# Mixer weights of a hybrid layer: both rounded parts of each strip stored in scratch memory in the first block and loaded from there in the later blocks

## The chip, the cores and the metric

One core of a Trainium2 chip runs the whole kernel. The metric is device time in microseconds (us); lower is better. TensorE (PE) does the matmuls and VectorE (DVE), ScalarE (ACT) and GpSimd (POOL) the rest. SyncE's queue (SP) issues nearly all transfers, which 16 DMA engines carry.

## The reference, cut to what matters

A layer on 2048 tokens of width 1024, in float32: a normalisation, a projection by `w_in`, a convolution branch and a gated delta rule beside it, `w_out`, a feed-forward network and a last normalisation.

```python
h = adaln(x, g_norm_mix[layer], shift_m, scale_m)
p = h @ w_in[layer]                       # 1024 x 3592
gate_b, gate_c, h_conv, q, k, v, z, a, bt = jnp.split(p, split_at, axis=-1)
ya = gate_b * causal_depthwise_conv(gate_c * h_conv, conv_w_mix[layer])   # then a group norm
...                                       # q, k, v: convolution, silu, heads, l2 norm
o = chunked_gated_delta_rule(q, k, v, g_dec, beta)
y = jnp.concatenate([ya, yb], axis=-1) @ w_out[layer]
x = x + gate_m[:, None, :] * y
h = adaln(x, g_norm_ffn[layer], shift_f, scale_f)
gt, up = jnp.split(h @ w_gate_up[layer], 2, axis=-1)
x = x + gate_f[:, None, :] * ((jax.nn.silu(gt) * up) @ w_down[layer])
return adaln(x, g_norm_final, shift_o, scale_o)
```

## The kernel before, in words

**Products in parts.** A matrix product of float32 values is made of three matmuls in the type fp32r: each operand is cut into a rounded part `hi` and a rest `lo`, and hi·hi, hi·lo and lo·hi are summed in PSUM. Weights come in strips of 512 KB (128 partitions x 1024 values). `raw_w` (L382) loads a strip into `wraw` (4 buffers). `split_w` (L387) makes the two parts: ACT casts into `whi` (L389), DVE subtracts into `wlo` (L391). `whi` and `wlo` have 4 buffers each (the pool `wc`). The buffers of `wraw` also serve the modulation vectors (`mod_gen`, L460, which loads strips of `w_ada` one by one beside the other work, L465, and sums them on DVE, L467 and L469) and the second normalisation (`second_norm`, L579).

**The mixer.** It runs in 4 blocks of 512 tokens. A block uses 28 column strips of `w_in` (`col_strip`: k, q, v, z for four heads each, then 12 for the convolution branch), each for 24 matmuls of 512 columns in `proj` (L447), and then strips of `w_out` (`out_strip`): 8 of them in blocks 1 to 3, each for 24 matmuls. Block 0 goes through its 8 `w_out` strips twice, in two groups (`out_groups`, L406), with 12 matmuls a strip, so that the last two of its four token tiles come later. That is 152 strips in all, 36 of them different.

**Order of requests.** `requests` (L417) lists the strips of all four blocks. `next_w` (L443) keeps `PRE + 1` = 4 strips under way and hands out the first: when a strip is handed out, the third after it has been asked for. Block 0 begins apart: its first four strips are used a piece at a time, while the modulation of the next columns of the input is still being made from `w_ada` (`part_norm`, L798; `part_start`, L818; loads on L778; sums on DVE, L793 and L795; column sums on PE, L483).

**Order on the engines.** From the first k strip of block 0 to the end of the mixer, the order on each engine is planned: the class `Clock` (L54) follows all instructions with costs of its own, and `pin` (L201) fixes the order by the begin that it gives them. The chains of the delta rule (`head_chain`, `q_chain`, `chunk_chain`) and of the convolution branch (`mix_chain`, L1295; its cast is L1303) are put between the matmuls of the projections by it. An engine runs its instructions strictly in this order. SP too takes its transfers in order: one that waits for a buffer holds up all behind it.

**Behind the mixer** come the feed-forward network's two halves and its last product, with their own loads and splits. They have no pinned order.

Of the kernel before, what the change touches and what calls it, by code (L numbers as in the profile page):

```python
# [12 lines left out]
F32 = mybir.dt.float32  # L13
F32R = mybir.dt.float32r
# [6 lines left out]
P = 128  # L21
D = 1024
S = 2048
KD = D // P
# [186 lines left out]
def layer_kernel(ctx, tc, x, c, w_ada, b_ada, w_ada_final, b_ada_final, g_norm_mix, g_norm_ffn, g_norm_final,  # L211
                 w_in, conv_w_mix, conv_w_qkv, a_log, dt_bias, g_conv_out, g_dn_out, w_out, w_gate_up,
                 w_down, cst, out):
    nc = tc.nc
    x, out = x[0], out[0]
    w_ada, w_in, w_out, w_gate_up, w_down = w_ada[0], w_in[0], w_out[0], w_gate_up[0], w_down[0]
# [9 lines left out]
    wc = wctx.enter_context(tc.tile_pool(name="wc", bufs=4, side="left"))  # L226
    dr = ctx.enter_context(tc.tile_pool(name="dr", bufs=1, space=DRAM))
# [3 lines left out]
    def dense_ps():  # L231
        return pd.tile([P, 512], F32, name="pd")

    def misc_ps():
        return pm.tile([P, 512], F32, name="pm")
# [146 lines left out]
    def raw_w(src, shape, name="wraw"):  # L382
        raw = wr.tile(shape, F32, name=name)
        nc.sync.dma_start(raw, src)
        return raw

    def split_w(raw, shape):  # L387
        hi = wc.tile(shape, F32R, name="whi")
        nc.scalar.copy(hi, raw)  # L389
        lo = wc.tile(shape, F32R, name="wlo")  # L390
        (lo_engines.popleft() if lo_engines else nc.vector).tensor_sub(lo, raw, hi.bitcast(F32))  # L391
        return hi, lo
# [13 lines left out]
    def out_groups(b):  # L406
        if b:
            return [[(n, kp, range(CH)) for kp in KPS] for n in range(2)]
        return [[(n, kp, range(2 * g, 2 * g + 2)) for kp in order for n in range(2)]
                for g, order in enumerate((KPS, sorted(KPS)))]  # L410


    def strip_ahead():
        raw = [raw_w(w_gate_up[:, c0:c0 + P].rearrange("(k p) n -> p k n", p=P), [P, KD, P]) for c0 in (0, FF)]
        return raw, split_w(raw[0], [P, KD, P])

    def requests():  # L417
        for b in range(NB):
            for c0 in (2048, 1536, 2560, 3072):
                for h in range(NH):  # L420
                    yield col_strip, w_in, c0 + h * P
            for m in range(4):
                for c0 in (512, 1024, 0):
                    yield col_strip, w_in, c0 + m * P
            for g in out_groups(b):
                for n, kp, ts in g:
                    yield out_strip, n, kp
        yield strip_ahead,
    reqs, ready, bg = requests(), deque(), deque()

    def fill(n):
        while len(ready) < n:
            r = next(reqs, None)
            if r is None:
                break
            ready.append(r[0](*r[1:]))
            if bg:
                try:
                    next(bg[0])
                except StopIteration:  # L440
                    bg.popleft()

    def next_w():  # L443
        fill(PRE + 1)
        return ready.popleft()

    def proj(ps, w, hh, hl, ks=range(KD)):  # L447
        wh, wl = w
# [272 lines left out]
    with ExitStack() as actx:  # L721
# [29 lines left out]
        pre = []  # L751
# [64 lines left out]
                scale_split(ps, k, Gm, Sm, *hT)  # L816

        def part_start():  # L818
            pre.append((ready.popleft(), dense_ps()))
            clock.kept.add(pre[-1][1].name)  # L820

        def proj_ab(ps, ks):
# [7 lines left out]
        for h in range(NH):  # L830
            part_start()
            proj(pre[h][1], pre[h][0], *hT, ks=PARTS[0])
# [33 lines left out]
        for b in range(NB):  # L866
            hh, hl = hT
# [393 lines left out]
            for key, c0, dstT in (("k", 2048, kT), ("q", 1536, qT), ("v", 2560, None)):  # L1261
                clock.pinned = clock.pinned or key == "k"
                for h in range(NH):
                    m = (c0 - 1536) // P + h
                    if pre:
                        w, ps = pre.pop(0)
                        proj(ps, w, hh, hl, PARTS[2])
                        clock.kept.discard(ps.name)
                        fill(h + 1)
                    else:  # L1270
                        w, ps = next_w(), misc_ps() if b == 0 and key == "q" and h < 1 else dense_ps()
                        proj(ps, w, hh, hl)
                    take_now("cv", 1)
                    cv = cv_tile([P, BLK])
                    conv(cv, ps, [col["cw_qkv"][:, t * 12 + m:t * 12 + m + 1] for t in range(4)], halo[:, m, :])
                    nc.vector.tensor_copy(edge[:, m, :], ps[:, BLK - 3:])
                    nc.scalar.activation(cv if dstT is None else dstT[:, h, :], cv, AF.Silu)
                    done[key] += 1
                    if dstT is not None:
                        give("cv", 1)  # L1280
                    else:
                        spawn(v_chain(h, cv), 1)
# [4 lines left out]
            for h in range(NH):  # L1287
                w = next_w()
                ps = dense_ps()
                proj(ps, w, hh, hl)  # L1290
                nc.scalar.activation(zs[:, h, :], ps, AF.Silu)
                done["z"] += 1
# [26 lines left out]
            for m in range(4):  # L1319
                w = next_w()  # L1320
                pcg = dense_ps()
                proj(pcg, w, hh, hl)
                take_now("cv", 2)
                gc = cv_tile([P, BLK])
                nc.scalar.copy(gc, pcg)
                w = next_w()
                phc = dense_ps()
                proj(phc, w, hh, hl)
                nc.vector.tensor_mul(phc, phc, gc)
                give("cv", 1)  # L1330
                nc.vector.tensor_copy(uedge[:, m, :], phc[:, BLK - 2:])
                cv = cv_tile([P, BLK])
                conv(cv, phc, [col["cw_mix"][:, t * 4 + m:t * 4 + m + 1] for t in range(3)], uhalo[:, m, :])
                w = next_w()
                pgb = dense_ps()
                proj(pgb, w, hh, hl)
                nc.vector.tensor_mul(cv, cv, pgb)
                spawn(mix_chain(m, cv), 1)
# [288 lines left out]
    for hf in range(2):  # L1627
        m = 0
# [226 lines left out]
    for n, (g, s) in enumerate(items):  # L1855
# [9 lines left out]
        if g == 0:  # L1865
            for q in range(4):
                p = dense_ps()
                u, c0 = q // 2, q % 2
# [75 lines left out]
```

## Time and profile before

| what | value |
|---|---|
| time, median of 3 runs | 2406.51 us (2406.47 to 2407.99) |
| span of the profiled execution, first to last instruction | 2404.1 us |
| median less this span | 2.4 us |
| PE busy | 2342.0 us (97%) |
| DVE, ACT, POOL busy | 1779.7 (74%), 1050.3 (44%), 572.9 us (24%) |
| moved by DMA | 341.19 MB, mean 142 GB/s |

The span of the profiled execution is its own time; what lies around it in a run is the 2.4 us of the third row. A `group` row gives busy time and mean duration of one kind of instruction, and then how long its engine sat idle just before it and for whom. A `window` row gives, for a stretch of the span, its length and the busy time of PE, PE's weight loads, DVE, ACT and POOL with counts of instructions, then the granted TensorE clock (1.00 is full speed), the DMA engines' share and the rate. In a timeline, the row has start and duration, and in brackets the idle time before it and who ended it; "x8" is eight instructions merged.

### The profile page before, as it was taken

What the parts mean: (1) busy time and instruction counts of PE and PEld (TensorE: products, weight loads), DVE (VectorE), ACT (ScalarE), POOL (GpSimd) and SP (SyncE); (2) the same over time, 40 slices, a digit from 0 to 9 for tenths busy, and PEclk for the clock granted to TensorE, in tenths of its full rate; (3) what the DMA queues carried; (4) which work ended last, traced back from release to release, by engine and by line L of the source; (5) the groups of instructions that cost most, each with busy time, mean ns of one, the idle gap of its engine ahead of it and who ended that gap; (6) DMA issues with size and microseconds to landing.
All of it is one profiled execution on the core that took longest, in us unless ns stands there. A gap on an engine that the chain in (4) does not pass through costs nothing. (4 is left out here: it accounts for less than half of the span.)

```text
span 2404.1 us, 30949 instructions
## 1 busy us (share of the span) xinstructions
PE 2342.0 (97%) x11285; PEld 1938.6 (81%) x11285; DVE 1779.7 (74%) x2667; ACT 1050.3 (44%) x1787; POOL 572.9 (24%) x646
## 2 busy tenths in 40 slices
PE   7899999999999999999999999999999999999997
PEld 6788888887788888887888888878888877887786
DVE  5898879775977678788666556875656568878987
ACT  3644664444634564356543334433333323322345
POOL 0241344033513161111000000000000036434448
PEclk9999999999999999999999999999999999999999
DMA  7443565535553345255663334753433374333443
GB/s 252 119 119 92 169 191 164 148 106 166 145 141 122 115 141 146 61 155 161 215 209 116 101 104 122 247 161 90 129 99 105 104 247 154 121 108 119 136 138 142
DMA packets 400992, 341.19 MB, mean 142 GB/s; under 512 B 39796, under 2 KB 343165, under 8 KB 400775
## 3 DMA queue, kind: packets, MB, share of 16 engines
q1 hardware_dynamic: 399430, 337.01, 45.9%
q0 software_dynamic: 1152, 2.10, 0.6%
q8 instruction: 88, 1.44, 0.2%
q14 instruction: 66, 0.53, 0.1%
q10 hardware_dynamic: 256, 0.10, 0.0%
HBM read 265.74 MB, written 75.51 MB: 142 GB/s over the span
## 5 line engine op out<-in xcount | busy, mean ns | idle before, releaser
L389 ACT CAST whi<-wraw 128x1024 fp32r<-128x1024 f32 x286 | 299.7, 1049 | 394.1 <-PE pd L322 170.6
L391 DVE TENSOR_TENSOR wlo<-wraw,whi 128x1024 fp32r<-128x1024 f32 x286 | 360.3, 1261 | 102.7 <-ACT whi L389 100.0
L322 PE MATMUL pd<-hTh,whi 128*128 128x512 f32 x888 | 362.0, 409 | 0.6 <-ACT hTh L564 0.6
L322 PE MATMUL pd<-hTh,wlo 128*128 128x512 f32 x888 | 348.4, 392 | 1.0 <-DVE wlo L391 1.0
L322 PE MATMUL pd<-hTl,whi 128*128 128x512 f32 x888 | 348.2, 392 | 0.1
L322 PEld LDWEIGHTS pd<-hTh,wlo 128*128 128x128 f32 x888 | 167.7, 189 | 38.2 <-DVE wlo L391 1.4
L322 PEld LDWEIGHTS pd<-hTh,whi 128*128 128x128 f32 x888 | 168.5, 190 | 33.6 <-issue 1.0
L322 PEld LDWEIGHTS pd<-hTl,whi 128*128 128x128 f32 x888 | 168.3, 190 | 32.1 <-issue 1.0
L1606 POOL TENSOR_TENSOR wraw<-wraw 128x1024 f32<-128x1024 f32 x2 | 4.9, 2458 | 776.0 <-DMA wraw<-in_w_down_dram 776.0
L1554 DVE TENSOR_TENSOR sg<-sg,pd 128x512 f32<-128x512 f32 x44 | 30.2, 686 | 163.1 <-PE pd L322 163.1
L1812 DVE TENSOR_TENSOR acc<-acc,pd 128x512 f32<-128x512 f32 x192 | 127.3, 679 | 24.6 <-PE pd L322 23.8
L1692 ACT CAST xh<-ra 128x640 fp32r<-128x640 f32 (+1 forms) x85 | 60.4, 722 | 183.0 <-PE pm L322 137.3
L1239 DVE SCALAR_TENSOR_TENSOR cv<-pd,pcb,cv 128x511 f32<-128x511 f32 (+2 forms) x173 | 129.4, 748 | 5.2
L1701 POOL TENSOR_TENSOR xl<-ra,xh 128x640 fp32r<-128x640 f32 (+1 forms) x37 | 62.7, 1695 | 143.9 <-ACT xh L1692 133.7
L1812 DVE TENSOR_TENSOR acc<-acc,pm 128x512 f32<-128x512 f32 x120 | 81.6, 680 | 17.7 <-PE pm L322 17.2
L322 PE MATMUL pd<-whi,ym 128*128 128x512 f32 x256 | 84.8, 396 | 0.0
L1741 POOL TENSOR_TENSOR wraw<-wraw 128x512 f32<-128x512 f32 x40 | 68.8, 1743 | 47.1 <-DMA wraw<-in_w_down_dram 39.7
L322 PE MATMUL pd<-A22h,whi 128*128 128x512 f32 x176 | 68.9, 391 | 3.0 <-DVE sg L1554 3.0
L322 PE MATMUL pm<-S4h,whi 128*128 128x512 f32 x176 | 68.6, 390 | 1.4 <-ACT sg L1548 1.4
L322 PE MATMUL pd<-S2h,whi 128*128 128x512 f32 x176 | 68.6, 390 | 1.0 <-ACT whi L389 1.0
L322 PE MATMUL pd<-S2h,wlo 128*128 128x512 f32 x176 | 68.6, 390 | 0.5 <-DVE wlo L391 0.5
L322 PE MATMUL pd<-S3h,t3h 128*128 128x512 f32 x176 | 69.0, 392 | 0.0
(459 smaller groups left out, 6207.2 us busy)
## 6 DMA issues: line engine op xcount, KB each, us to landing
wraw<-in_w_in_dram SPq DMA_DIRECT2D x112, 512.0 KB, 4.6
wraw<-in_w_gate_up_dram SPq DMA_DIRECT2D x88, 512.0 KB, 3.9
ra<-act SPq DMA_DIRECT2D x80, 448.0 KB, 3.6
wraw<-in_w_out_dram SPq DMA_DIRECT2D x40, 512.0 KB, 3.6
act<-S SPq DMA_DIRECT2D x80, 256.0 KB, 3.5
act<-act SPq DMA_DIRECT2D x68, 256.0 KB, 2.7
wraw<-in_w_ada_dram SPq DMA_DIRECT2D x32, 512.0 KB, 4.2
wraw<-in_w_down_dram SPq DMA_DIRECT2D x22, 512.0 KB, 4.3
```

The source lines that it names most:

```text
L322: mm(*args, **kw)
L389: nc.scalar.copy(hi, raw)
L391: (lo_engines.popleft() if lo_engines else nc.vector).tensor_sub(lo, raw, hi.bitcast(F32))
L1239: nc.vector.scalar_tensor_tensor(cv[:, n - t:], u[:, :BLK - n + t], taps[t], cv[:, n - t:], op0=ALU.mult, op1=ALU.add)
L1554: nc.vector.tensor_add(s5[i], s5[i], a[i])
L1606: nc.gpsimd.tensor_mul(r, r, first_w["gate"])
L1692: nc.scalar.copy(hi, raw[:, c0:c1, :])
L1701: eng.tensor_sub(lo, raw, hi.bitcast(F32))
L1741: nc.gpsimd.tensor_mul(r[:, hs], r[:, hs], gate_f[:, hs])
L1812: nc.vector.tensor_add(accs[s, u][:, ns], accs[s, u][:, ns], ps)
```

## The change

In block 0 each of the 36 strips is still loaded, cast and subtracted. When it is handed out, both parts are also written to scratch memory in DRAM (`put_by`, two stores of 512 KB). Whenever a strip comes again, in block 0's second `w_out` group and in blocks 1 to 3, `part_load` loads the two parts straight into `whi` and `wlo`: no raw strip, no cast and no subtraction, and two loads of 512 KB instead of one. Both kinds of transfer are issued on SP. The first four strips are stored in `part_start`. The feed-forward network's weights are left as they were.

```diff
+    def part_load(key):
+        tiles = []
+        for name, src in zip(("whi", "wlo"), parted[key]):
+            t = wc.tile([P, D], F32R, name=name)
+            nc.sync.dma_start(t.bitcast(F32), src)
+            tiles.append(t)
+        return tiles
+
+    def parts_of(key, make, *args):
+        k, n = (KD, P) if make is col_strip else (2, 512)
+        if key in parted:
+            return [t.rearrange("p (k n) -> p k n", n=n) for t in part_load(key)]
+        tiles = make(*args)
+        parted[key] = [dr.tile([P, D], F32, name=f"parted{len(parted)}_{e}") for e in "hl"]
+        stores[id(tiles)] = tiles, parted[key]
+        return tiles
...
-                    yield col_strip, w_in, c0 + h * P
+                    yield parts_of, c0 + h * P, col_strip, w_in, c0 + h * P
...
-                    yield out_strip, n, kp
+                    yield parts_of, (n, kp), out_strip, n, kp
...
+    def put_by(w):
+        tiles, dst = stores.pop(id(w), ((), ()))
+        for t, d in zip(tiles, dst):
+            nc.sync.dma_start(d, t.rearrange("p k n -> p (k n)").bitcast(F32))
+        return w
+
     def next_w():
         fill(PRE + 1)
-        return ready.popleft()
+        return put_by(ready.popleft())
...
-            pre.append((ready.popleft(), dense_ps()))
+            pre.append((put_by(ready.popleft()), dense_ps()))
```

The lines behind L412 stand 24 to 27 lines later in the changed kernel (L778 becomes L805, L1303 becomes L1330). The stores are L467 there, the loads of parts L419.

The order moves at three places. The first is SP's queue in the first microseconds, before the pinned order begins: behind the four raw strips stood the `w_ada` loads for the second part of the modulation (`yah`, `yal` and `ym` are the buffers that they go to).

```order
L384 DMA wraw<-in_w_in_dram 128x8x128 x4
L778 DMA yah<-in_w_ada_dram 128x384 x4
L778 DMA yal<-in_w_ada_dram 128x384 x4
L778 DMA ym<-in_w_ada_dram 128x384 x8
L836 DMA wab<-in_w_in_dram 128x8x8
```

In the changed kernel the eight stores of the first four strips stand between them (`parted_h` and `parted_l` are the scratch tensors of the two parts).

```order
L384 DMA wraw<-in_w_in_dram 128x8x128 x4
L467 DMA parted_h<-whi 128x1024
L467 DMA parted_l<-wlo 128x1024
L467 DMA parted_h<-whi 128x1024
L467 DMA parted_l<-wlo 128x1024
L467 DMA parted_h<-whi 128x1024
L467 DMA parted_l<-wlo 128x1024
L467 DMA parted_h<-whi 128x1024
L467 DMA parted_l<-wlo 128x1024
L805 DMA yah<-in_w_ada_dram 128x384 x4
L805 DMA yal<-in_w_ada_dram 128x384 x4
L805 DMA ym<-in_w_ada_dram 128x384 x8
```

The sixteen `w_ada` loads are now issued only when DVE has made the fourth strip's `wlo`.

The second place is ACT in block 1, at the first cast of the convolution branch (`lv<-cv`, L1303 before). Before, casts of strips (`whi<-wraw`) stand all around it.

```order
L389 CAST whi<-wraw 128x1024 x2
L1301 ACTIVATE cv<-cv 128x512
L389 CAST whi<-wraw 128x1024
L1325 COPY cv<-pd 128x512
L389 CAST whi<-wraw 128x1024
L1303 CAST lv<-cv 128x512
L389 CAST whi<-wraw 128x1024
L1310 ACT_TABLE_LOAD
```

Now (L1330) none of them is left, and the delta rule's last copies (`lv<-pm`) have come ahead of it.

```order
L1352 COPY cv<-pd 128x512
L1103 COPY lv<-pm 128x512 x4
L1119 COPY lv<-pm 64x4x64 x4
L1128 COPY lv<-pm 64x4x64 x4
L1239 ACTIVATE junkd,so<-ch 128x128 x4
L1328 ACTIVATE cv<-cv 128x512
L1330 CAST lv<-cv 128x512
```

So on ACT nothing here waits for a weight strip any more, and the planner has chosen another order for the chains.

The third place is SP's queue at block 0's second `w_out` group. Before, the raw strips (`wraw`) stand ahead of the block's results (`x_0` and `x_1` are token tiles of the result in DRAM, `cb` is a piece of the input).

```order
L384 DMA wraw<-in_w_out_dram 128x2x512 x7
L1392 DMA x_0_107<-cv 128x512
L1387 DMA cb<-in_x_dram 128x512
L1392 DMA x_1_108<-cv 128x512
L1387 DMA cb<-in_x_dram 128x512
L384 DMA wraw<-in_w_out_dram 128x2x512
L1392 DMA x_0_107<-cv 128x512
```

Now most of the loads of parts, each of which waits until PE has let go of a buffer, stand between the results.

```order
L1419 DMA x_0_107<-cv 128x512
L1414 DMA cb<-in_x_dram 128x512
L419 DMA whi<-parted_h 128x1024
L419 DMA wlo<-parted_l 128x1024
L1419 DMA x_1_108<-cv 128x512
L1414 DMA cb<-in_x_dram 128x512
L419 DMA whi<-parted_h 128x1024 x2
L419 DMA wlo<-parted_l 128x1024 x2
L419 DMA whi<-parted_h 128x1024
L419 DMA wlo<-parted_l 128x1024 x2
L1419 DMA x_0_107<-cv 128x512
```

A load of parts now waits for results of DVE and POOL that stand ahead of it, and the results wait for PE.

More of the change, by code (lines that the diff above doesn't have):

```diff
@@ L410, in out_groups @@
                 for g, order in enumerate((KPS, sorted(KPS)))]
+    parted = {}
+    def part_load(key):
[13 more added lines that the diff above has]
+        return tiles
+    stores = {}
     def strip_ahead():
@@ L420, in requests @@
                 for h in range(NH):
-                    yield col_strip, w_in, c0 + h * P
+                    yield parts_of, c0 + h * P, col_strip, w_in, c0 + h * P
             for m in range(4):
                 for c0 in (512, 1024, 0):
-                    yield col_strip, w_in, c0 + m * P
+                    yield parts_of, c0 + m * P, col_strip, w_in, c0 + m * P
             for g in out_groups(b):
                 for n, kp, ts in g:
-                    yield out_strip, n, kp
+                    yield parts_of, (n, kp), out_strip, n, kp
         yield strip_ahead,
```

## The prediction

> **What bounds the kernel now.** I read the busy times first, then stretches of the span, then PE's waits. The page says that PE is the bound, and what one strip's two parts cost on the other engines:
>
> ```profile
> span 2404.1 us, 30949 instructions
> PE 2342.0 (97%) x11285; PEld 1938.6 (81%) x11285; DVE 1779.7 (74%) x2667; ACT 1050.3 (44%) x1787; POOL 572.9 (24%) x646
> ...
> L389 ACT CAST whi<-wraw 128x1024 fp32r<-128x1024 f32 x286 | 299.7, 1049 | 394.1 <-PE pd L322 170.6
> L391 DVE TENSOR_TENSOR wlo<-wraw,whi 128x1024 fp32r<-128x1024 f32 x286 | 360.3, 1261 | 102.7 <-ACT whi L389 100.0
> ```
>
> The windows split the span at about the ends of the start, of block 0, and of the mixer:
>
> ```profile
> 0.00:45.00 45.00, 28.19 (x119) 24.68 (x120) 22.21 (x45) 18.35 (x27) 4.81 (x17) 0.97 0.90 290
> ...
> 250.00:300.00 50.00, 47.98 (x263) 40.15 (x261) 40.14 (x45) 38.27 (x64) 17.73 (x26) 1.00 0.60 196
> 300.00:1090.00 790.00, 781.73 (x4205) 653.36 (x4204) 615.16 (x1032) 395.62 (x767) 244.28 (x325) 0.99 0.48 139
> 1090.00:2404.00 1314.00, 1285.67 (x5653) 1057.15 (x5651) 927.49 (x1237) 503.20 (x738) 251.21 (x205) 0.99 0.45 142
> ```
>
> From 300 to 1090 us PE idles for 790 - 781.73 = 8.3 us only. The matmuls stay, so work removed from DVE and ACT can return no more than such idle time and the slow matmuls behind it. PE's waits there, longest first:
>
> ```profile
> PE pm L510 <- ACT junkd L912: 3.8, 1, 3.8
> PE pm L1307 <- ACT lv L1303: 2.3, 1, 2.3
> ```
>
> Two waits hold 6.1 of the 8.3 us. The timeline of the one on L1303:
>
> ```profile
> 451.90 1.04 ACT L389 CAST whi<-wraw 128x1024 fp32r<-128x1024 f32 x1 [3.94 <-DMA wraw<-in_w_in_dram]
> 452.85 0.61 ACT L1303 CAST lv<-cv 128x512 fp32r<-128x512 f32 x1
> ...
> 453.51 0.50 PE L1307 MATMUL pm<-lv,gones_r 128*128 128x512 f32 x1 [2.35 <-ACT lv L1303]
> ```
>
> A strip's cast stood first in ACT's queue, waited 3.94 us for its raw transfer, and held up the cast on which PE waited. The other wait, in ACT's and PE's rows:
>
> ```profile
> 656.86 1.03 ACT L389 CAST whi<-wraw 128x1024 fp32r<-128x1024 f32 x1
> ...
> 658.20 2.07 PE L510 MATMUL pm<-wraw,ones_r 128*128 128x512 f32 x2 [3.79 <-ACT junkd L912]
> ...
> 660.93 0.63 PE L322 MATMUL pd<-hTh,wlo 128*128 128x512 f32 x1
> 661.36 0.63 PE L322 MATMUL pd<-hTh,whi 128*128 128x512 f32 x1
> ```
>
> Here too a strip's cast lies just ahead of what PE waits for, and behind the wait matmuls begin 0.43 us apart (661.36 - 660.93). Undisturbed it is 0.23 us:
>
> ```profile
> 470.44 0.39 PE L322 MATMUL pd<-hTh,whi 128*128 128x512 f32 x1
> 470.67 0.39 PE L322 MATMUL pd<-hTl,whi 128*128 128x512 f32 x1
> ```
>
> The windows behind both waits show it as granted clock, 0.66 and 0.63:
>
> ```profile
> 455.00:460.00 5.00, 5.00 (x30) 4.91 (x30) 4.90 (x9) 4.07 (x6) 0.00 (x0) 0.66 0.81 231
> ...
> 660.00:665.00 5.00, 5.00 (x18) 3.94 (x17) 4.89 (x10) 1.52 (x2) 0.34 (x1) 0.63 0.52 131
> ```
>
> So a wait costs its length and 5 x (1 - 0.66) = 1.7 or 5 x (1 - 0.63) = 1.9 us more. The first comes to 2.35 + 1.7 = 4.1 us, the second to 3.79 + 1.9 = 5.7 us, about 10 together. The Trainium skill, in "TensorE: Matmul & The Clock Gate", Part 1, says that PE's clock is halved after an idle window of about 3.4 us; by that rule the wait of 2.35 us need not have cost clock. The trace agrees for the longer wait, and 0.66 behind the shorter one says that less can be enough.
>
> **The change part by part.** All 152 strips but the 36 first ones lose cast and subtraction: 116 x 1.049 = 122 us of ACT and 116 x 1.261 = 146 us of DVE. 108 of them lie in blocks 1 to 3. Matmuls that PE performs anyway hide all of it, so it counts nothing by itself. Its worth is in the waits: ACT no longer has a raw transfer or a strip's cast in front of the two. Their order is planned anew as well. I take both as gone: -10. The bounds are 0, if others of the same size take their place, and -12, the two and the 8.3 - 6.1 = 2.2 us of small ones. What is late next is PE's own matmul, that is the next strip.
>
> At the start, the eight stores hold SP until the fourth `wlo` exists. The rows for SP, DVE and PE:
>
> ```profile
> 21.55 2.82 SPq L778 DMA_DIRECT2D yah<-in_w_ada_dram  x4
> ...
> 26.70 3.78 SPq L778 DMA_DIRECT2D ym<-in_w_ada_dram  x8
> ...
> 31.44 1.22 DVE L391 TENSOR_TENSOR wlo<-wraw,whi 128x1024 fp32r<-128x1024 f32 x1
> ...
> 33.17 0.41 DVE L793 TENSOR_SCALAR zs<-yah,cs 128x384 f32<-128x384 f32 x1
> ...
> 42.45 0.61 DVE L795 SCALAR_TENSOR_TENSOR gate_m<-ym,cs,gate_m 128x384 f32<-128x384 f32 x1
> ...
> 43.21 1.43 PE L483 MATMUL pm<-ones_r,gate_m 128*128 128x16 f32 x6 [2.67 <-DVE gate_m L795]
> ```
>
> The fourth `wlo` ends at 31.44 + 1.22 = 32.7, so `yah` is issued at about 33.1 instead of 21.55, 11.5 us later. Before, it lay ready when DVE came to it at 33.17. A transfer of this kind (the second row; the first is a raw strip's) lands after 3.3 us:
>
> ```profile
> wraw<-in_w_in_dram SPq DMA_DIRECT2D x112, 512.0 KB, 4.6
> ...
> ym<-in_w_ada_dram SPq DMA_DIRECT2D x16, 192.0 KB, 3.3
> ```
>
> So DVE starts at 36.4. Its 16 sums then take (starts 36.32 to 42.45 hold twelve steps of about 0.53) 16 x 0.53 = 8.5 us, to about 45; PE begins 45.2 - 43.2 = 2 us later. If the stores' 4.2 MB hold up the ring, issues stay at 2.82 / 4 = 0.7 us each, and the last lands at 33.1 + 16 x 0.7 + 3.3 = 47.6: 5 us later. The lower bound is 1, the 3.2 us of DVE's later start less about 2 us of sums of the third part that are now planned behind. I take 2.5, near the DVE rows. The third part's loads come later too, and are covered by PE's matmuls on the second.
>
> In the rest of block 0, each strip brings 1.05 MB of stores. They wait on SP for the same casts that its raw loads wait for already:
>
> ```profile
> SPq L384 <- DVE wlo L391: 666.7, 166, 19.9
> ```
>
> Behind them on SP are the next raw strip and `w_ada` piece. The tight place is the second `w_out` group. A strip there holds 12 matmuls, 12 x 0.23 = 2.8 us, in which its 1.05 MB must arrive: 375 GB/s. The DMA rows:
>
> ```profile
> 28.00:30.00 2.00, 1.75 (x3) 1.01 (x4) 1.72 (x3) 2.00 (x4) 0.00 (x0) 1.00 1.06 387
> ...
> 284.00:309.00 25.00, 23.91 (x113) 19.32 (x112) 19.49 (x21) 13.99 (x18) 7.29 (x5) 1.00 0.81 258
> ...
> 30.00:36.00 6.00, 6.00 (x23) 4.79 (x22) 5.89 (x10) 2.58 (x5) 0.32 (x1) 1.00 0.92 292
> ```
>
> 387 GB/s is what full engines moved; 292 is the nearest stretch at 0.92. The group's window (284 to 309) already moves 258 x 25 = 6.5 MB; with nine strips of 1.05 for ten raw ones of 0.52 it would be 10.7 MB, 27.6 us at 387 GB/s. That is 2.6 us over, against three strips asked for ahead, 8 us less a landing of 4.6 (the raw strip's row), a lead of 3.4. I take +1 here, for all of block 0; bounds -2, as the 250 to 300 window holds 2.0 us of waits which a relieved DVE may end, and +8 (rival 2). The Trainium skill, in "DMA: Bandwidth & Descriptors", Where 436 GB/s comes from, gives about 358 GB/s as one core's share of HBM, which would speak against the change: an estimate from it is 2.9 us a strip, a loss of 1 us more. The 387 of the row is above that, so the row decides.
>
> In blocks 1 to 3 a strip takes 24 x 0.23 = 5.5 us and side work, and 1.05 MB in 5.5 us is 190 GB/s; the window shows 0.48 of the engines busy now, so there is room. A load waits on SP for PE's last use of the buffer, three strips ahead of its own use (16 us), and the raw strip's 4.6 us of landing fit in that three times.
>
> What is new is that PE's progress holds SP: behind each load are `w_ada` pieces for DVE, and the delta rule's round trips through DRAM. An order with other misses of the planner will have waits of its own. The rows give 0 (much slack on DVE and ACT) to 10 us (as many as now); I take 4, one wait like the smaller of the two. The 188 further issues on SP are off the path. The network behind the mixer keeps its code and order: 0.
>
> Sum on the profiled execution: 2404.1 - 10 + 2.5 + 1 + 4 = 2401.6 for the span. The median lies 2.4 us above this span, so 2404.0 against 2406.5, -0.1%.
>
> **The rivals.** Rival 1, faster: the relief is whole, with no new wait (-10 + 2.5 + 1 - 1 = -7.5, 2399.0). For it: DVE falls by 108 x 1.261 = 136 of 615 us in blocks 1 to 3, and ACT then waits for no raw strip. Against: SP is now tied to PE.
>
> Rival 2, slower: block 0 is bound by DMA, because stores and loads together don't reach the 387 GB/s but the 292. It decides as soon as a strip's 1.05 MB take longer than its 2.8 us by more than the lead: 3.6 us at 292, 8 x 0.8 = 6.4, and 1.3 MB of others 4.5, less the lead of 3.4: +7.5. The start would then cost 5. In all -10 + 5 + 7.5 + 4 = +6.5, 2413. For it: DMA is at 0.90 already in the first 45 us. Against: rows of 4 KB in place of the 512-byte pieces of `w_in`.
>
> Rival 3, no gain: the two waits are replaced one for one, so start and block 0 are added: -10 + 2.5 + 1 + 10 = +3.5, 2410. The pinned order speaks for it, the lighter queues against.
>
> **How the numbers follow.** A measurement tells about 0.2% (4.8 us) from no change. My forecast, 2404, has a chance of 0.45; with its terms' bounds it spreads over about 2398 to 2409, and 0.17 of the 0.45 lie below 2406.5 - 4.8 = 2401.7. Rival 1 has 0.2, rival 2 0.2, rival 3 0.15, of which 0.05 lie above 2411.3. Faster: 0.17 + 0.2 = 0.37. Slower: 0.2 + 0.05 = 0.25. Same, the rest: 0.28 + 0.10 = 0.38. The range takes rival 1 with its bound (-12 + 1 - 1 = -12, 2395) and rival 2 to 2414.
>
> **What would show it.** Right: in blocks 1 to 3 no cast of strips, DVE near 480 us and PE's idle time under 5 us; PE's L483 of the second part at about 45.7; PE's idle time in the second `w_out` group under 2 us. Wrong: PE waits on `whi` or `wlo` behind a DMA in many places, or L483 at 48 (rival 2); a new wait of 3 us or more on ACT or DVE in blocks 1 to 3 for each that went (rival 3); PE faster or slower behind 1100 us, which I hold at 0.

## The result, and the profile after

| what | before | after |
|---|---|---|
| time, median of 4 runs each on one chip | 2407.25 us (2406.47 to 2408.22) | 2426.71 us (2420.22 to 2428.28) |
| ratio after to before, 95% interval | | 1.0072 [1.0059, 1.0085] |
| span of the profiled execution | 2404.1 us | 2418.1 us |

The change makes the kernel 19.5 us slower by the medians. The profiled execution of the changed kernel is the fastest of its four, so the traces compared here show 14.0 us of it.

The page of the changed kernel, busy time and transfers:

```profile
span 2418.1 us, 30933 instructions
...
PE 2338.8 (97%) x11285; PEld 1935.3 (80%) x11285; DVE 1650.8 (68%) x2551; ACT 932.2 (39%) x1666; POOL 556.2 (23%) x646
...
DMA packets 348701, 439.75 MB, mean 182 GB/s; under 512 B 42803, under 2 KB 260156, under 8 KB 348486
...
L389 ACT CAST whi<-wraw 128x1024 fp32r<-128x1024 f32 x170 | 178.5, 1051 | 278.1 <-PE pm L322 145.8
L391 DVE TENSOR_TENSOR wlo<-wraw,whi 128x1024 fp32r<-128x1024 f32 x170 | 210.3, 1238 | 48.8 <-ACT whi L389 46.7
...
whi<-parted_h SPq DMA_DIRECT2D x116, 512.0 KB, 4.0
wlo<-parted_l SPq DMA_DIRECT2D x116, 512.0 KB, 5.8
```

The change did what it says: 116 casts and subtractions are gone (286 to 170), DVE is 129 us less busy and ACT 118, and DMA moves 98.6 MB more. PE has as many matmuls as before and waits more.

To see where, I cut the span at four matmuls that both kernels have: the column sums of the second part of the start (`gate_m`, L483, now L510), the first `w_out` matmul on `yah` in block 0, the first in block 1, and the last in block 3. (At the start `yah` is a buffer for `w_ada`; in the blocks a tile of the same name holds a rounded part of the mixer's output.) PE's rows of the kernel before (its first is in the prediction, 43.21):

```profile
250.34 0.48 PE L322 MATMUL pd<-whi,yah 128*128 128x512 f32 x1
...
527.00 0.39 PE L322 MATMUL pd<-whi,yah 128*128 128x512 f32 x1
...
1099.32 0.39 PE L322 MATMUL pd<-whi,yah 128*128 128x512 f32 x1
```

and of the changed kernel:

```profile
50.49 1.43 PE L510 MATMUL pm<-ones_r,gate_m 128*128 128x16 f32 x6 [4.81 <-DVE gate_m L822]
...
262.55 0.47 PE L322 MATMUL pd<-whi,yah 128*128 128x512 f32 x1
...
549.61 0.39 PE L322 MATMUL pd<-whi,yah 128*128 128x512 f32 x1
...
1114.22 0.39 PE L322 MATMUL pd<-whi,yah 128*128 128x512 f32 x1
```

The differences give five stages. The table below uses the same cuts for every experiment; each entry is the stage's length less that of the kernel before, in us.

| kernel | start, to 43.21 | strips of block 0, 207.1 | passage to block 1, 276.7 | to the end of block 3, 572.3 | behind the mixer, 1304.8 | median less before's |
|---|---|---|---|---|---|---|
| after | +7.3 | +4.9 | +10.4 | -7.7 | -0.9 | +19.5 |
| first four strips unstored | +0.1 | +6.7 | +4.8 | -7.1 | +3.1 | +6.3 |
| x1's load on POOL's queue | +7.2 | +6.8 | +9.5 | -2.4 | +2.4 | +20.6 |
| loads only | +0.2 | 0.0 | +9.0 | -7.2 | +3.0 | +0.9 |
| stores only | +7.2 | +6.4 | +1.9 | -1.2 | +3.8 | +16.2 |
| second group made | +7.3 | +8.5 | +5.2 | -8.3 | +2.3 | +13.8 |
| stores on POOL's queue | +4.6 | +11.5 | +8.1 | -6.7 | +2.2 | +18.0 |
| stores only, an eighth | +4.8 | -0.2 | +0.2 | -2.0 | +1.4 | +4.4 |
| stores only, half | +6.5 | +1.9 | -0.4 | -1.2 | +6.9 | +6.8 |
| stores only, not of the strips | +7.4 | +6.5 | +0.8 | -0.5 | +3.3 | +15.6 |
| stored in block 1 | +0.1 | -1.2 | +25.8 | -4.7 | +1.9 | +18.1 |
| loads only, second group made | -0.1 | -1.0 | +3.4 | -7.6 | +2.1 | -3.2 |
| first four unstored, second group made | +0.2 | +5.2 | +10.2 | -6.9 | +3.9 | +9.4 |

The code behind the mixer is the same in all; its spread, 1303.9 to 1311.7 us, says how finely single traces can be compared. Stages are read from one trace each: that of the half is of an execution at 2419.56 us, 5.8 above its median, and that of the last row of one at 2418.35, 2.3 above. So only differences of several us, or seen in several kernels, are used.

**The start.** SP's rows: the last store is issued at 32.83, and only then the `w_ada` loads, as foreseen. The four `yah` loads take 4.02 us to issue where they took 2.82. DVE's rows show that it waits once for a transfer, 5.53 us, and for what PE then waits:

```profile
32.83 0.32 SPq L467 DMA_DIRECT2D parted_l<-wlo  x1
33.20 4.02 SPq L805 DMA_DIRECT2D yah<-in_w_ada_dram  x4
```

```profile
38.92 0.42 DVE L820 TENSOR_SCALAR zs<-yah,cs 128x384 f32<-128x384 f32 x1 [5.53 <-DMA yah<-in_w_ada_dram]
...
41.52 2.58 DVE L822 SCALAR_TENSOR_TENSOR zs<-yal,cs,zs 128x384 f32<-128x384 f32 x4
...
45.72 0.16 DVE L831 TENSOR_TENSOR Gm<-pm,pca 128x3 f32<-128x3 f32 x1 [1.28 <-PE pm L510]
...
46.45 3.89 DVE L822 SCALAR_TENSOR_TENSOR gate_m<-ym,cs,gate_m 128x384 f32<-128x384 f32 x6
```

From 38.92 to 50.35 us no sum waits for a transfer, but the sixteen take 11.4 us. Before, most sums into `zs` and `gate_m` alternated, about 0.53 us apart; here those into `zs` come first and then those into `gate_m`, about 0.65 us apart, and a wait of 1.28 us for PE's column sums lies between.

**The strips of block 0.** Windows of before and after, to the first `yah` matmul, and then PE's waits in the first 300 us of after (total us, times, longest):

```profile
60.00:250.00 190.00, 183.41 (x987) 151.97 (x986) 166.41 (x294) 89.19 (x182) 54.57 (x73) 0.99 0.39 105
```

```profile
60.00:262.00 202.00, 190.08 (x1019) 156.59 (x1019) 167.97 (x298) 88.55 (x182) 56.65 (x73) 0.99 0.75 245
```

```profile
PE pm L510 <- DVE gate_m L822: 10.2, 2, 5.4
PE pm L510 <- DVE zs L822: 6.6, 1, 6.6
...
PE pm L1335 <- DVE lv L1331: 4.4, 1, 4.4
```

DMA works at 245 GB/s, a share of 0.75 in the mean, and still PE waits: 4.4 us for `lv`, for which it has no wait in this stage before. In the chain that ends last, transfers stand ahead of it (the rows are start, duration, what).

```profile
106.11 5.95 DMA wraw<-in_w_in_dram
112.16 1.05 ACT whi L389
...
155.60 7.32 DMA dm<-Dg
...
163.51 6.79 DMA yal<-dm
```

The last two are the delta rule's round trip through DRAM, for which DVE waits. Before and after:

```profile
159.12 0.21 DVE L1032 TENSOR_TENSOR lv<-yal 128x31 f32<-128x31 f32 x1 [3.74 <-DMA yal<-dm]
```

```profile
170.39 0.21 DVE L1059 TENSOR_TENSOR lv<-yal 128x31 f32<-128x31 f32 x1 [9.42 <-DMA yal<-dm]
```

SP issues `dm` before at

```profile
150.79 0.37 SPq L1018 DMA_DIRECT2D dm<-Dg  x1
```

so from there it takes 159.12 - 150.79 = 8.3 us before and 170.39 - 155.60 = 14.8 us after. What stands behind on DVE comes later, among it `lv` (L1331), for which PE waits 4.4 us at 199 us.

The mean hides that the engines are full just there. Windows over the raw strip of 106 us and over the two steps of the round trip, after:

```profile
106.00:112.00 6.00, 6.00 (x34) 5.11 (x33) 5.89 (x10) 2.11 (x3) 1.29 (x1) 1.00 0.96 279
155.00:163.00 8.00, 8.00 (x51) 7.00 (x50) 4.93 (x6) 3.78 (x15) 4.52 (x7) 1.00 1.03 320
163.00:171.00 8.00, 8.00 (x43) 6.74 (x42) 0.54 (x3) 3.60 (x14) 3.01 (x6) 1.00 0.95 289
```

and over the round trip before:

```profile
150.00:159.00 9.00, 9.00 (x58) 7.83 (x57) 5.38 (x6) 4.69 (x20) 4.01 (x7) 1.00 0.85 205
```

Cut into slices of 5 us from 60 us to about the first `yah` matmul, 19 of 40 have a DMA share of 0.9 or more; before it is 1 of 38.

**The passage to block 1.** PE's longest waits from 297 us to block 1's first `yah` matmul, and windows:

```profile
PE pd L322 <- DMA whi<-parted_h: 3.8, 1, 3.8
PE pd L322 <- DMA wlo<-parted_l: 2.8, 2, 2.0
```

```profile
298.00:328.00 30.00, 22.40 (x88) 16.65 (x86) 5.71 (x9) 2.35 (x4) 7.18 (x8) 0.94 0.99 381
...
322.00:328.00 6.00, 1.51 (x6) 0.69 (x4) 1.13 (x2) 0.00 (x0) 3.23 (x5) 1.00 1.02 406
```

Here the engines are full (0.99 at 381 GB/s, up to 406), and PE waits for the strips themselves, 6.6 us in all. In block 1 the 2.3 us on L1303 are gone, but 2.0 us of waits on ACT's `cv` (L1304, for PE's L933) have come.

**Blocks 1 to 3.** From the first `yah` matmul of block 1 the stage is 7.7 us shorter. PE's busy time in about the same stretch, before and after:

```profile
527.00:1099.00 572.00, 566.31 (x3003) 471.52 (x3002) 435.81 (x722) 286.52 (x546) 167.28 (x223) 0.99 0.45 129
```

```profile
550.00:1114.00 564.00, 561.27 (x2999) 469.49 (x2997) 348.24 (x643) 208.41 (x465) 152.49 (x219) 1.00 0.62 205
```

Idle time falls from 5.7 to 2.7 us; the wait on `junkd` is gone. The other 5.0 us by which the stretch is shorter are PE's busy time, for nearly as many matmuls in the trace (3003 and 2999), at a granted clock of 0.99 before and 1.00 after. Of the 2.7 us most is one wait, which was 0.3 us before:

```profile
PE pm L933 <- ACT kq L1304: 1.9, 1, 1.9
```

### The profile page after: what moved, and what is told of

It reads as the page before. It is cut to its first block, busy times and chain, and to the rows that moved or that the text cites. A ratio compares the mean times of both kernels' runs of the same rounds, so it can differ in the third digit from the quotient of the medians.

```text
span 2418.1 us, 30933 instructions
## 1 busy us (share of the span) xinstructions
PE 2338.8 (97%) x11285; PEld 1935.3 (80%) x11285; DVE 1650.8 (68%) x2551; ACT 932.2 (39%) x1666; POOL 556.2 (23%) x646
## 4 chain that ended last, share of the span: by engine, by line
PE 68%; DVE 14%; DMA 8%; ACT 3%; issue 3%; POOL 2%; SPq 1%; DVEq 0%; ACTq 0%; POOLq 0%
PE pd L322 43%; PE pm L322 17%; DVE cv L1266 2%; DVE acc L1839 1%; DVE wlo L391 1%; DVE lv L1059 1%; DVE yal L1061 1%; DMA y<-xT 1%; DMA dm<-Dg 1%; DMA yal<-dm 1%; PE pm L1108 1%; DVE cv L1264 1%; POOL wraw L1768 1%; PE pm L1100 1%; DMA A12d<-y 1%
## 5 line engine op out<-in xcount | busy, mean ns | idle before, releaser
L389 ACT CAST whi<-wraw 128x1024 fp32r<-128x1024 f32 x170 | 178.5, 1051 | 278.1 <-PE pm L322 145.8
L391 DVE TENSOR_TENSOR wlo<-wraw,whi 128x1024 fp32r<-128x1024 f32 x170 | 210.3, 1238 | 48.8 <-ACT whi L389 46.7
L1839 DVE TENSOR_TENSOR acc<-acc,pm 128x512 f32<-128x512 f32 x120 | 81.7, 681 | 18.5 <-PE pm L322 18.1
L1338 DVE RECIPROCAL cv<-cv 128x512 f32<-128x512 f32 x16 | 53.6, 3352 | 22.6 <-ACT cv L1337 22.5
```

Of the source, the lines that this page charges most:

```text
L1338: nc.vector.reciprocal(sy, sy)
L1839: nc.vector.tensor_add(accs[s, u][:, ns], accs[s, u][:, ns], ps)
```

## The experiments

Formed from the trace: the stores cost the start and block 0's strips, and together with the loads the passage. What the experiments are to decide is how: by the order of SP's queue, in which a store waits for its cast and holds all behind it, or by bytes on shared DMA engines; and which of it the reloads cost alone. "Theory A" and the rivals in the texts on record are each run's own. All diffs are against the changed kernel.

**First four strips not stored.**

```diff
+        if next(serial) < 4:
+            return make(*args)
         tiles = make(*args)
```

> The changed kernel, but the first four strips, made before the loop, are not stored: they are made again in block 1 and stored there, for blocks 2 and 3. Theory A (the eight stores on SP's queue at 23.5 to 32.8 us hold back the loads behind them, and that is the whole of the 5.6 us by which block 0's head came later): the column sums L510 of the second part come back from 50.5 to about 43 to 45 us, the head transposes of block 0 from 72.2 to 67 us, and the time falls by about 5 to 2415. Rival (the start is late for another reason, or the time is given back at a later bound in block 0, whose strips wait for DMA anyway): head earlier but the last yah matmul of block 0 still at 312 to 313 us, time 2419 to 2421.

Measured: 2413.73 us, ratio to before 1.0022 [1.0013, 1.0031]. The column sums are at 43.27, as before, so the eight stores are the whole cost of the start. The strips still cost 6.7 us. The 13 us off the changed kernel are more than the theory gave: the passage too is 5.6 us better here.

**The second norm's load on POOL's queue.**

```diff
-            nc.sync.dma_start(xt, x1d[b * CH + i])
+            nc.gpsimd.dma_start(xt, x1d[b * CH + i])
```

> The changed kernel, with second_norm's load of x1 issued on POOL's queue and not on SP's. Theory A (in the passage from block 0 to block 1 SP stands some 8 us before this load, which waits for its own store to land, and the loads of the last strip stand behind it): the waits of 3.83 and 0.82 us for whi and wlo at 327 us go, block 1's first yah matmul comes 4 to 8 us earlier than 549.6, time 2413 to 2416. Rival (the passage is bound by bytes, some 400 GB/s, and the order of the queue is of no account): the same idle time at 300 to 335 us under other names, time 2419 to 2421.

Measured: 2428.02 us, 1.0079 [1.0067, 1.0092]. Theory A fails: the load is out of SP's way, and PE still waits for both parts in the same place, with the engines full, as the rival has it (its time was too low). PE's rows and the window:

```profile
326.35 0.51 PE L322 MATMUL pd<-whi,ym 128*128 128x512 f32 x1 [2.31 <-DMA whi<-parted_h]
327.59 0.50 PE L322 MATMUL pd<-wlo,ym 128*128 128x512 f32 x1 [0.74 <-DMA wlo<-parted_l]
```

```profile
322.00:328.00 6.00, 2.95 (x12) 1.89 (x12) 1.38 (x2) 0.00 (x0) 3.22 (x5) 1.00 1.02 416
```

**Loads only**, `one_pair` being one pair of scratch tensors.

```diff
-        parted[key] = [dr.tile([P, D], F32, name=f"parted{len(parted)}_{e}") for e in "hl"]
-        stores[id(tiles)] = tiles, parted[key]
+        parted[key] = one_pair
+        if len(parted) == 5:
+            stores[id(tiles)] = tiles, one_pair
```

> Loads without stores: one strip alone (the fifth) is stored, and all 116 later uses load that pair, so the later uses multiply by the wrong weights; instructions and loaded bytes are those of the changed kernel, 70 of its 72 stores are left out. Theory A (the stores cost the 16 us up to the last yah matmul of block 0, 313.3 against 297.1, and with the loads together the 6 us of the passage to block 1): block 0 as in the kernel before, last yah at 297 to 301, passage to block 1 at most 2 us late, gains of blocks 1 to 3 kept: time 2395 to 2400. Rival (the reloads alone cost the passage, since each use then needs 1 MB instead of 0.5): block 1's first yah 6 to 10 us later than in the kernel before, time 2403 to 2408.

Measured: 2408.4 us, 1.0004 [0.9995, 1.0012]. The rival is right: without stores block 0 costs nothing up to the first `yah` matmul, but the passage still costs 9.0 us. Its window has DMA near full without a store of parts (results still go out):

```profile
298.00:328.00 30.00, 25.70 (x104) 18.16 (x102) 3.45 (x5) 0.00 (x0) 5.85 (x7) 0.94 0.96 361
```

So even with stores for nothing the scheme would only break even. All these loads read one pair of scratch tensors; whether 36 pairs would land as fast isn't tested.

**Stores only.**

```diff
         if key in parted:
-            return [t.rearrange("p (k n) -> p k n", n=n) for t in part_load(key)]
+            return make(*args)
```

> Stores without loads: both parts of each strip are stored in block 0 as in the changed kernel, but blocks 1 to 3 make their strips again from the raw weights, as the kernel before does. Theory A (stores are the cost): first yah of block 0 at 262 (250.3 before), last at 309 to 313 (297.1 before), the later blocks as before, time 2407 plus 12 to 16: 2419 to 2423. Rival (the loads that run among the stores from block 0's second group on are the cost): time 2411 to 2414, of which the start is 5.6.

Measured: 2423.66 us, 1.0066 [1.0052, 1.008]. Start +7.2, strips +6.4, and no gain later, as theory A has it (its time 0.7 us too low). The stores are the larger half of the cost. With loads-only this separates the stages: stores make start and strips late, reloads the passage.

**Second group of block 0 made again.**

```diff
-                    yield parts_of, (n, kp), out_strip, n, kp
+                    yield (parts_of, (n, kp), out_strip, n, kp)[2 if b == 0 and ts[0] else 0:]
```

> The changed kernel, but the second w_out group of block 0 makes its strips again from the raw weights, as before; the scratch is loaded from block 1 on. A strip of that group is used for 12 matmuls only (2.5 us), and loading it takes 1 MB where making it takes 0.5 MB. Theory A (the reloads of this group and of the first strips of block 1, 386 to 416 GB/s at a full DMA share at 298 to 328 us also in the loads-only run, cost 9 us by themselves): block 0 up to 262 us as in the changed kernel, from the last yah of block 0 to the first of block 1 229 to 231 us (236.3 in the changed kernel, 230.0 in the one before), time 2416 to 2420. Rival (it is block 1's own reloads that are late, and whatever stands ahead of them is of no account): 236 us as in the changed kernel, time 2424 to 2428.

Measured: 2421.24 us, 1.0056 [1.0042, 1.007]. By my table the passage is 5.2 instead of 10.4 us late. From last to first `yah`, as the expectation has it, it takes 234.5 us (313.46 to 547.91), between the two theories, as does the time. About half the passage's cost hangs on the reloads for 12 matmuls; the medians (13.8 against 19.5 us over the kernel before) agree.

**Stores on POOL's queue.**

```diff
-            nc.sync.dma_start(d, t.rearrange("p k n -> p (k n)").bitcast(F32))
+            nc.gpsimd.dma_start(d, t.rearrange("p k n -> p (k n)").bitcast(F32))
```

> The changed kernel with its 72 stores issued on POOL's queue and not on SP's: the bytes stay, but SP no longer stands at a store until the cast behind it is done, with the raw loads of the next strips waiting behind. Theory A (the stores cost by the order of SP's queue): ACT's waits for wraw (22.8 us, 10 times, at 60 to 300 us) go back towards 7.1, the head of block 0 to 66.8 to 68 us, first yah of block 0 at 251 to 256 (262.5 in the changed kernel), time 2412 to 2419. Rival B (they cost by their bytes, a DMA share of 0.75 to 0.87 in place of 0.43 to 0.48): first yah stays at 259 to 263, time 2423 to 2428.

Measured: 2425.49 us, 1.0073 [1.0061, 1.0085]; first `yah` at 266.44. The time is rival B's, the first `yah` later than either said. Theory A fails here too, though not cleanly, since POOL's own work now stands behind the stores. The start is the cleaner piece: `yah` is issued at 21.75, as early as before, and the column sums are still 4.6 us late. SP's row shows the issue, and the row of the DMA issues in the first 60 us how such transfers land:

```profile
21.75 2.82 SPq L805 DMA_DIRECT2D yah<-in_w_ada_dram  x4
```

```profile
ym<-in_w_ada_dram SPq DMA_DIRECT2D x16, 192.0 KB, 7.5
```

7.5 us to land, against 3.3 in the kernel before, with SP's order untouched. From 20 to 45 us the DMA share is 1.07 here and 0.90 before, and DVE now waits for `ym` and `kd`, 0.56 to 1.93 us at a time.

**Stores of an eighth, and of half of the bytes**, both without loads.

```diff
-            nc.sync.dma_start(d, t.rearrange("p k n -> p (k n)").bitcast(F32))
+            nc.sync.dma_start(d[:, :P], t.rearrange("p k n -> p (k n)")[:, :P].bitcast(F32))
```

(`512` in place of `P` for the half.)

> Stores without loads, as in the run of that kind, but each store writes 128 of the 1024 columns (64 KB and not 512): as many stores at the same places of SP's queue, an eighth of the bytes. Theory A (order of SP's queue: SP still waits for each cast): as with whole stores, first yah of block 0 at 260 to 264, time 2420 to 2424. Rival B (bytes): first yah at 251 to 253, time 2408 to 2411. Both at work: between them, 2412 to 2418.

> Stores without loads, each store writing 512 of the 1024 columns: as many stores at the same places, half of the bytes. With an eighth of the bytes the median was 4.4 us over the kernel before, with all of them 16.2. Theory L (each byte delays what shares the DMA engines, in proportion): 4.4 plus 3/7 of 11.8, so 2414 to 2418, first yah of block 0 at 258 to 260. Rival T (bytes cost only once the DMA share comes near 0.9): 2410 to 2413, first yah at 255 to 257.

Measured: 2411.87 us, 1.002 [1.0011, 1.0029], for an eighth; 2413.77 us, 1.0029 [1.0016, 1.0042], for half. The eighth's time lies between rival B's range and that of both at work. Its first `yah` is at 254.88 instead of 251 to 253, since its start is 4.8 us late: nearly the order of SP's queue alone (with an eighth of the bytes; its first `yah` load is issued at 30.19 already, between the stores). Its strips cost nothing (-0.2 us), although SP waits at as many stores for as many casts. With half of the bytes they cost 1.9 and with all 6.4 us. ACT's waits for raw strips follow the bytes; from 60 to 250 us, in the order none, an eighth, half and all (stores only):

```profile
ACT whi L389 <- DMA wraw<-in_w_in_dram: 7.1, 7, 2.0
```

```profile
ACT whi L389 <- DMA wraw<-in_w_in_dram: 11.1, 7, 3.5
```

```profile
ACT whi L389 <- DMA wraw<-in_w_in_dram: 13.9, 8, 4.1
```

```profile
ACT whi L389 <- DMA wraw<-in_w_in_dram: 19.4, 10, 5.4
```

(total us, times, longest). So in the strips it is bytes. The 5-us slices with a DMA share of 0.9 or more follow them too: 1 of 38, 1 of 39, 4 of 40 and 20 of 41. Whether the cost grows in proportion or faster isn't settled: half's time, 2413.8, lies just under theory L's 2414 and over T's 2413, and its interval holds both; its first `yah`, at 258.71, is where L has it, but in the execution that took 2419.56 us.

**Stores that are not of the strips.** The same bytes from a resident tile, from the fifth strip on.

```diff
+            s = t.rearrange("p k n -> p (k n)").bitcast(F32)
-            nc.sync.dma_start(d, t.rearrange("p k n -> p (k n)").bitcast(F32))
+            nc.sync.dma_start(d if len(parted) < 8 else d.rearrange("p (a n) -> p a n", a=2), s if len(parted) < 8 else ck[:, :512].unsqueeze(1).to_broadcast([P, 2, 512]))
```

> Stores without loads, 72 of 512 KB at the same places of SP's queue, but from the fifth strip on what is stored is a resident tile of constants and not the strip: SP waits for no cast there and no strip buffer is held until its store has landed; the bytes stay. Theory B (bytes: the DMA engines are shared, so raw strips and the scan's round trip land later): first yah of block 0 at 260 to 264 and the last at 309 to 314, time 2419 to 2424, as with the strips themselves stored. Rival (the wait for the cast on SP, or the buffers held): first yah at 256 to 258 (start alone), time 2411 to 2415.

Measured: 2422.3 us, 1.0057 [1.0044, 1.007]; strips +6.5 us, as with the strips themselves. Neither SP's wait for a cast nor a buffer held until its store has landed is needed for the cost. With the eighth this leaves bytes. How they reach PE differs, though: the round trip takes 10.0 us here (162.65 to 172.68) and not 14.8, and PE waits 1.2 us on `lv`. So the late round trip is the way in the changed kernel, and not the only one; 24 of 41 slices are at 0.9 or more.

**Stored in block 1 instead.**

```diff
+        uses[key] = uses.get(key, 0) + 1
+        if uses[key] <= (1 if make is col_strip else 2):
+            return make(*args)
```

> Strips are made in block 0 as in the kernel before, made again and stored in block 1, and loaded in blocks 2 and 3. Theory A (block 0 costs because its start, its weights for the modulation and its half-size w_out groups leave DMA and SP no room; the gain of 7.7 us lies in block 2): block 0 and the passage to block 1 as before (first yah of block 1 at 527 to 529), block 1 at most 4 us longer, block 2 7 us shorter, time 2399 to 2406. Rival (a strip stored is late wherever it is, as its store holds SP): first to last yah from block 0's end to block 1's end longer by 6 to 12 us, time 2406 to 2413.

Measured: 2425.61 us, 1.0076 [1.0064, 1.0089]. Both expectations were too low: the passage and block 1 cost 25.8 us. From 297 to 552 us PE is busy for 236.51 of 255 us and the granted clock falls to 0.95; DMA is at 0.80, near the 0.75 of block 0 in the changed kernel (23 of 51 slices at 0.9 or more; before, 6 of 46 from 297 to 527):

```profile
297.00:552.00 255.00, 236.51 (x1254) 196.56 (x1253) 189.95 (x326) 113.64 (x228) 76.04 (x103) 0.95 0.80 268
```

So block 0 isn't special: in both places tried, stores beside strips that are being made cost more than the loads give back.

**Loads only, second group made; and both edits on the real kernel.** The edits are those shown above, taken together.

> The loads-only kernel (one stored pair is read by all later uses, whose weights are so wrong), with block 0's second w_out group made again and not loaded: the scheme without its stores and without the reloads that feed 12 matmuls. Theory: the passage from block 0 to block 1 as in the kernel before (229 to 231 us from last to first yah, 238.7 with those loads), gain of block 2 kept: time 2399 to 2403. Rival (the first reloads of block 1 are late whatever stands ahead): 236 to 239 us, time 2406 to 2409.

> The changed kernel with both edits at once: the first four strips stored in block 1, block 0's second w_out group made again. Theory (the two costs add: 13.0 and 5.5 us by the medians of the runs alone): 2406 to 2410, no faster than the kernel before. Rival (they recover the same time, as both ease block 0's end): 2412 to 2415.

Measured: 2403.5 us, 0.9989 [0.998, 0.9997], and 2416.07 us, 1.0032 [1.0021, 1.0044]. Without stores and without the short reloads the passage is 3.4 us late (233.4 us from last to first `yah`, in between the expectations again), and the kernel is 3 us under the one before: what is left to gain if stores were free. For the real kernel the median lies just above the rival's range and is no better than with the first edit alone. But the twelve times fall apart, five at 2405.2 to 2411.1 and seven at 2416.0 to 2419.0 us, so whether the two edits add isn't settled. In the traced execution (2418.35) the passage is 10.2 us late for another reason. With raw strips again in the second group, a cast on ACT waits for its strip, the subtraction follows, and behind it on DVE stands the sum (`cv`, L1416) that frees PE's bank; DVE's row, PE's row and the window:

```profile
292.62 1.23 DVE L391 TENSOR_TENSOR wlo<-wraw,whi 128x1024 fp32r<-128x1024 f32 x1 [3.23 <-ACT whi L389]
```

```profile
296.50 0.80 PE L322 MATMUL pd<-whi,yah 128*128 128x512 f32 x1 [5.01 <-DVE cv L1416]
```

```profile
294.00:302.00 8.00, 5.50 (x17) 4.52 (x18) 5.60 (x8) 5.41 (x9) 2.55 (x2) 0.61 0.76 239
```

A wait of 5.01 us and, in the window with it, a clock of 0.61. No kernel that multiplies by the true weights beats the kernel before by its median.

## Why the prediction was wrong

I forecast 2404.0 us, no change; it is 2426.7, slower, and outside the range (2395 to 2414). By the terms of the sum:

- **The gain, -10: right in kind, smaller by what blocks 1 to 3 lost at their head.** Both waits are gone. From block 1's first `yah` matmul on, the loads bring -7.7 us, and -6.7 to -8.3 in six other kernels that load; kernels without loads have -0.5 to -2.0. The kernel with the second norm's load on POOL's queue is the exception (-2.4), and where the strips are stored in block 1 (-4.7) only two blocks load. The wait on L1303 was in block 1's earlier part, where it is outweighed by the waits on `whi`, `wlo` and ACT's `cv`.
- **The start, +2.5 (1 to 5): 7.3, beyond my upper bound.** The issue at 33.1 was right (33.20). Two steps failed. The transfer "lands after 3.3 us" was taken from a row without the stores; it took 5.7, and DVE began at 38.92 and not at 36.4. And "16 x 0.53 = 8.5 us" was the step of sums that alternate between two accumulators; in the order that came they took 11.4 us, with 1.28 us of waiting for PE in it, and not one waited for a later transfer. An eighth of the bytes in the same order costs 4.8 us, whole stores on another queue 4.6, both together 7.3.
- **The rest of block 0, +1 (-2 to +8): +4.9 for the strips alone, and then the passage.** The step that failed is the treatment of stores as a matter of SP's queue ("They wait on SP for the same casts that its raw loads wait for already") and of rate in one group only: for the strips ahead of it the stores' bytes were put at nothing. The queue was indeed harmless there: the eighth and the resident tile show it. But 37.7 MB of stores (36 x 1.05) filled the engines in half of the 5-us slices, at a mean share of 0.75, and made others' transfers slower: the round trip from 8.3 to 14.8 us, ACT's waits for strips from 7.1 to 22.8 us.
- **The second group, in the same +1:** the place and the kind were right, the size wrong. 381 to 406 GB/s were there, as taken, but demand goes on beyond the group: its last reloads, block 1's first, the results and the `w_ada` strips all fall into 298 to 328 us. The loads alone cost 9.0 us from the first `yah` of block 0 to the first of block 1, of which making the second group again takes away 5.6 (9.0 to 3.4). The lead of 3.4 us didn't cover that.
- **New waits in blocks 1 to 3, +4 (0 to 10):** behind block 1's first `yah` two, of 1.9 and 0.5 us, on ACT for PE's L933, which are inside the -7.7; the others lie at block 1's head and are counted with the passage.
- **Behind the mixer, 0:** -0.9 us, within the spread of that stage.

Of the rivals, the second (block 0 bound by DMA, 2413) was nearest, and its mechanism, full engines, is at work in the strips and in the passage. Its rate of 292 GB/s didn't come in the passage, where the rate was as high as forecast; in the strips the three full windows above moved 279 to 320 GB/s, near it. The Trainium skill, in "DMA: Bandwidth & Descriptors", Where 436 GB/s comes from, has 358 GB/s as a core's share; the 406 of the row shows more here, so that figure doesn't explain the passage either.

What the profile was to show came in part: no strip casts in blocks 1 to 3, DVE at 483.8 us from 300 to 1090 us ("near 480"), PE's idle time 2.7 us from 550 to 1114. But PE idles 7.6 us from 298 to 328 us, about the second `w_out` group, which was to stay under 2. Of the signs of being wrong came L483's matmul later than "45.7" and later than rival 2's "48", and waits on `whi` and `wlo` behind a DMA, though few.

Open: how the cost of the strips grows with the bytes; whether the two savings add; the profiled execution is 6.5 us under the median of its runs, and no trace shows where those lie (the stage behind the mixer, the shortest of all here, may hold part of them); why leaving the start's stores out also eases the passage by 5.6 us, where the planned order differs too.

## What to carry to other kernels

Saving work on engines that are off the path pays only the waits that they cause and the slow matmuls behind these, here 8 us in 2400; price the transfers that replace it by every landing someone waits for (the next strip, a round trip through DRAM), not by whether the mean rate suffices. A mean DMA share hides full stretches: here it went from 0.39 to 0.75, and the slices at 0.9 or more from 1 in 38 to 19 in 40. And before storing something for reuse, compare the bytes of a reload with the work done per load: here a strip used for 12 matmuls could not be reloaded in time at twice its size.

## What the runs showed of the hardware

- Landing times grew where the engines were full: a 192 KB transfer (median of 16) from 3.3 to 7.5 us with stores on another queue, the DMA share from 20 to 45 us going from 0.90 to 1.07; and the two-step round trip from 8.3 us at a share of 0.85 to 14.8 us at 1.03 and 0.95, in a stage whose mean is 0.75.
- An eighth of the bytes in as many stores left the strips' stage unchanged (-0.2 us): issuing them and SP's waits at them cost nothing that this trace can show.
- The transfers of the passage reached 406 GB/s at a share of 1.02 over 6 us, and 416 with x1's load on POOL's queue.
- A wait of 5.01 us goes with a granted clock of 0.61 in the 8 us around it; on the 5.50 us in which PE was busy there that is 5.5 x 0.39 = 2.1 us more, by my estimate.
